# Token-shift differences on VectorE alone, and the low-rank additions behind the last receptance operand, in an RWKV-7 / NSA step

## The chip, the cores and the metric

The kernel runs on one core of a Trainium2 chip. The metric is the device time of one execution in microseconds (us). Three runs of the kernel before took 994.48, 988.21 and 993.82 us, the median is 993.82. Besides these there is one profiled execution, from which all times of single instructions come.

Engine names as in the profile: PE is TensorE (PEld its weight loads), DVE is VectorE, ACT is ScalarE, POOL is GpSimd, SP is SyncE, which issues the DMAs.

## The reference, cut to what matters

Two layers of a decoder: an RWKV-7 layer and a native-sparse-attention layer, on 512 prompt tokens and 8 x 4 sample tokens, with 1024 channels. The change lies in the first layer's beginning:

```python
hp = rms_norm(xp, norm_w[i])
prev = jnp.concatenate([shift[:, None, :], h[:, :-1]], axis=1)
xx = prev - h                                           # token shift
xr, xw, xk, xv, xa, xg = [h + xx * mu[i] for i in range(6)]
r, k, v, z = jnp.einsum('pbtc,pcd->pbtd', jnp.stack([xr, xk, xv, xg]), w_rkvz)
w = -jax.nn.softplus(-(w0 + jnp.tanh(xw @ w1) @ w2)) - 0.5    # decay
a = jax.nn.sigmoid(a0 + (xa @ a1) @ a2)                       # rate
```

After it come the recurrence over time, the gate and the output projection, and then the attention layer. Both layers' outputs and states are returned.

## The kernel before, in words

**Layout.** Activations lie with channels on the 128 partitions, in eight tiles (k = 0 to 7), and the 544 tokens along the free axis, in two halves of 272 (256 prompt tokens and 16 sample tokens each).

**Split operands.** A full-precision product is made of three products of reduced operands: each operand is a high part and a low part. `operand` (L320) calls `split` (L293): ScalarE copies the raw tile into the high part (L298), and an engine of the caller's choice subtracts it from the raw tile to give the low part (L299). `products` (L329) then runs, for every channel tile k, three matmuls a half (L337): high weight with high operand, high weight with low operand, low weight with high operand. That is 48 matmuls for an output tile of 128 channels, and those of tile k need both parts of tile k. Weights are split in the same way (`weight`, L302), their low part by GpSimd, VectorE or both in halves, as the plan's letters say (p, v, h).

**The start of layer 0** (`layer0`, L472). `rstd` (L404) computes the norm factor `rs` of every token. `low_rows` (L422) multiplies the low-rank weights of the decay and the rate straight with the raw input, once for a token's own row and once for the row before it (L446, L448), and copies the products out of PSUM on ScalarE (L452, L454). It returns a function `rows` (L456), called `hid()` in `layer0`, that finishes them on VectorE: both multiplied with `rs` (L460), and the shifted one added to the other (L461 for the prompt tokens, L462 for the first token of the second half, L465 for each of the two groups of eight sample tokens that take the given state, L466 and L467 for the other sample tokens). The result `self.hid` is read by `rates` (L604): `stack_tanh` (L538) and `stack_copy` (its first reader is L549 on ScalarE).

Then, for each channel tile k, `shifted(k)` (L507): VectorE makes the normalised tile (L510), ScalarE copies its sample tokens and writes the two edge columns (L513, L515, L516), **VectorE or GpSimd takes the difference of neighbouring tokens (L514)**, and VectorE takes the sample tokens' differences (L517). The plan's entry `shp` names the tiles whose L514 is done by GpSimd: 1, 3, 5 and 7. `mix("r", k)` (L524, VectorE) gives the receptance's mixture, and `operand(..., nc.vector)` splits it (L298 on ScalarE, L299 on VectorE).

**The loop over the eight receptance tiles** (m, from L629) loads the weights, runs `project` and copies the result out (L637). Woven into it are, at m = 1, the compression of the sample caches (`sample_pages`, L577: `cmp_bias`, L1496, with its matmuls L1505; `cmp_sample`, L1540, with its matmuls L1553 on pages that are loaded by DMA; and `cmp_hidden`, L1512, whose addition L1519 follows the copy L1517, whose product L1522 ends the hidden layer and goes to the matmul L1529); after m = 2 the call `hid()`; after each m some calls of `inputs` (L595), two each after m = 0 and m = 1, which make the mixtures of key, value and gate for a tile (L524 three times), split the first (L298, L299) and send the others to DRAM (L599); and from m = 4 the steps of `rates`.

**What sets the order.** Each engine runs its instructions in a fixed order. That order is worked out when the kernel is built, with estimated durations, from the program's order as priority: an instruction that comes later in the program may be placed ahead of an earlier one where the estimate says that the earlier one isn't ready. So the additions of `hid()`, and mixtures of `inputs`, stand on VectorE among the work on the receptance's operands, though the program names them after it. Temporary tiles come from pools of a fixed number of buffers: 8 for the raw tiles and `rs` (tag `d`), 16 for the split operands of the receptance (tag `x`), 16 shared by the key's operands and the two copies that `hid()` works on (tag `t`).

`with tc.issue_after(ins):` adds, to each instruction made in the block that runs on the engine of `ins`, an ordering behind `ins` on that engine.

Of the kernel before, what the change touches and what calls it, by code (L numbers as in the profile page):

```python
# [9 lines left out]
F32 = mybir.dt.float32  # L10
# [3 lines left out]
OP = mybir.AluOpType  # L14
# [19 lines left out]
    'FS': 4,  # L34
    'VS': (0, 0, 1, 1, 1, 1, 1, 3),
    'IV': (0, 0, 0, 0, 4, 6, 6, 0),
    'shp': (1, 3, 5, 7),
    'CS': 1,
    'FT': 1,
    'WR': 'pppvhphh',  # L40
# [186 lines left out]
class K:  # L227
# [65 lines left out]
    def split(self, raw, hi, lo, eng=None, first=None):  # L293
        nc = self.nc
        if first:
            first.tensor_copy(hi, raw)
        else:
            nc.scalar.activation(hi, raw, AF.Copy)  # L298
        (eng or nc.gpsimd).tensor_tensor(lo, raw, hi.bitcast(F32), OP.subtract)  # L299
        return hi, lo  # L300

    def weight(self, src, cols, eng=None, tag="w"):  # L302
# [96 lines left out]
    @staticmethod  # L399
    def h2(t):  # L400
        return t.rearrange("p (h n) -> p h n", h=2)
# [70 lines left out]
    def layer0(self, ctx):  # L472
        nc, I, O = self.nc, self.I, self.O
# [19 lines left out]
        for j in range(2):  # L493
            raw = self.t("p", (128, 4, 128))
# [12 lines left out]
        def shifted(k):  # L507

            h = self.t("p")
            nc.vector.scalar_tensor_tensor(h, X[k], self.V("nw0", k), rs, op0=OP.mult, op1=OP.mult)  # L510
            dx = self.t("p")
            a, d = h2(h), h2(dx)
            nc.scalar.activation(steps[:, k, 8:40].rearrange("p (h n) -> p h n", h=2), a[:, :, HP:HN], AF.Copy)  # L513
            (nc.gpsimd if k in PLAN["shp"] else nc.vector).tensor_tensor(d[:, :, 1:HP], a[:, :, 0:HP - 1], a[:, :, 1:HP], OP.subtract)  # L514
            nc.scalar.activation(d[:, 0, 0:1], a[:, 0, 0:1], AF.Copy, scale=-1.0)  # L515
            nc.scalar.activation(d[:, 1, 0:1], a[:, 1, 0:1], AF.Identity, scale=-1.0, bias=a[:, 0, HP - 1:HP])  # L516
            nc.vector.tensor_tensor(d[:, :, HP:HN], steps[:, k, 0:32].rearrange("p (h n) -> p h n", h=2),  # L517
                                    steps[:, k, 8:40].rearrange("p (h n) -> p h n", h=2), OP.subtract)
            H.append(h)
            DX.append(dx)  # L520

        def mix(n, k):
            raw = self.t("d")
            nc.vector.scalar_tensor_tensor(raw, DX[k], self.V("m" + n, k), H[k], op0=OP.mult, op1=OP.add)  # L524
            return raw
# [29 lines left out]
        def samp(dst, src, eng):  # L555
            d = dst.rearrange("p (h n) -> p h n", h=2)
            if eng is nc.scalar:
                nc.scalar.activation(d, src, AF.Copy)
            else:
                eng.tensor_copy(d, src)  # L560

        self.open(kctx, t=16, rst=1)
        hid = self.low_rows(low, X, sh, rs)
        Xr, Xk = [], []
        for k in range(KT):
            shifted(k)
            Xr.append(self.operand(mix("r", k), nc.vector))

        self.sums, self.center = (self.c0(n, (128, 128), F32R) for n in ("sums", "center"))
        self.mean = self.c("mean", (128, 128), F32R)  # L570
# [6 lines left out]
        def sample_pages():  # L577
            with ExitStack() as cctx:
                self.open(cctx, side="right", cw=1, cl=2, ca=3)
                if not PLAN["PT"]:  # L580
                    self.pages()
                if PLAN["PO"] == 0:
                    self.page_rows()
                self.cmp_weights(lambda shape: self.reg["cw"].tile(list(shape), F32, name=self.nm("cw")))
                if PLAN["PO"] == 1:
                    self.page_rows()
                self.cmp_bias()
                if PLAN["PO"] == 2:
                    self.page_rows()
                self.cmp_sample()  # L590
# [4 lines left out]
        def inputs(m):  # L595

            Xk.append(self.split(mix("k", m), self.t("t", dt=F32R), self.t("t", dt=F32R), nc.vector))
            for n in "vg":
                nc.sync.dma_start(spilled[n][:, m], mix(n, m))  # L599
            nc.scalar.activation(ps[:, m:m + 1], h2(H[m])[:, 1, HP - 1:HP], AF.Copy)  # L600
# [28 lines left out]
        for m in range(KT):  # L629
            if m == PLAN["CS"]:  # L630
                sample_pages()
            if m == 4:
                self.open(w2ctx, side="right", w2=8, st2=2)
            w = ahead[m] if m < len(ahead) else self.weight(I["rkvz"][0, m], 128, WE["WR"][m])
            pt = self.project(w, Xr)
            r = self.t("p")
            nc.scalar.activation(h2(r), pt[:, :, :HN], AF.Copy)  # L637
            samp(arS[:, m, 1], pt[:, :, HP:HN], nc.scalar)
            R.append(r)
            if m == 2:  # L640
                hid()
            for _ in range(PLAN["INP"][m]):
                inputs(len(Xk))
            if m >= 4:
                for _ in range(PLAN["RT"][m]):
                    next(rate, None)
# [1598 lines left out]
```

## Time and profile before

| | us |
|---|---|
| runs | 994.48, 988.21, 993.82 (median 993.82) |
| profiled execution, its own time | 999.77 |
| its span, first to last instruction | 997.8 |
| PE busy | 944.5 (95%) |
| DVE busy | 658.8 (66%) |
| ACT busy | 561.0 (56%) |
| POOL busy | 424.0 (42%) |
| mean granted TensorE clock | 0.974 |

How to read the rows: a row of the view in order of time has the start, the duration of the row, the engine, the source line, the operation, output and inputs, and how many instructions it merges; in brackets stands how long the engine was idle before it and what released it. A merged row's duration runs from its first start to its last end. Source lines can be those of a helper: L299 is the low part of a split, L337 a matmul of `products`. A row of the view by stretches has the stretch, its length, the busy time of PE, PEld, DVE, ACT and POOL with the number of instructions, the granted clock as a share, the DMA engines' share and GB/s. A row of the view by groups has the count, total busy time in us, the mean in ns, and the idle time before with its releasers.

### The profile page before, as it was taken

How to read it: one execution, taken by the hardware profiler on the slowest of the kernel's cores; microseconds unless marked ns; L12 is line 12 of the kernel's file. 1: busy time of each engine (PE TensorE's matmuls, PEld its weight loads, DVE VectorE, ACT ScalarE, POOL GpSimd, SP SyncE). 2: the span in 40 equal slices, each digit the busy share in tenths (PEclk: the TensorE clock that was granted, in tenths of full speed). 3: DMA queues.
4: the chain of work that ended last, by engine and by line, in shares of the span. 5: the costliest groups of instructions: out<-in, count | busy, mean ns of one | idle time of the engine just before them, and what ended most of it. 6: DMA issues, size and time to landing. Idle time of an engine off the chain costs nothing.

```text
span 997.8 us, 24773 instructions
## 1 busy us (share of the span) xinstructions
PE 944.5 (95%) x9445; PEld 845.5 (85%) x9445; DVE 658.8 (66%) x1525; ACT 561.0 (56%) x1366; POOL 424.0 (42%) x496
## 2 busy tenths in 40 slices
PE   8899999998899999999999888999999999998997
PEld 7899999988887788888879878999788888787896
DVE  6976679897847442556977624755786556569664
ACT  5455786665253353555554645656685668566552
POOL 4414646553411533421222765655343537442431
PEclk9799999999899997999999989999999999999999
DMA  5486236669374454663574795332454342555634
GB/s 191 136 274 215 87 118 188 186 192 273 112 209 117 139 138 139 208 180 94 164 222 131 247 242 168 110 109 80 123 127 136 104 123 82 155 157 187 187 103 157
DMA packets 149239, 157.46 MB, mean 158 GB/s; under 512 B 52226, under 2 KB 97058, under 8 KB 148866
## 3 DMA queue, kind: packets, MB, share of 16 engines
q1 hardware_dynamic: 149122, 155.90, 51.9%
q8 instruction: 74, 1.21, 0.5%
q14 instruction: 43, 0.35, 0.1%
HBM read 112.25 MB, written 43.80 MB: 156 GB/s over the span
## 4 chain that ended last, share of the span: by engine, by line
PE 51%; DVE 12%; DMA 7%; ACT 7%; issue 4%; POOL 3%; SPq 1%; DVEq 0%; POOLq 0%; ACTq 0%
PE ph L337 23%; PE pq L1821 4%; PE pw L1915 3%; PE pq L1899 3%; PE pr L1235 2%; DMA w<-in_win 2%; DMA d<-dram 2%; ACT l L298 2%; POOL l L299 1%; DVE tmp L1137 1%; DMA w<-in_rkvz 1%; PE ph L2167 1%; PE ph L382 1%; ACT a L1855 1%; PE s L1269 1%
## 5 line engine op out<-in xcount | busy, mean ns | idle before, releaser
L337 PE MATMUL ph<-x,l 128*128 128x272 f32 x2412 | 352.7, 297 | 6.8 <-DVE bs L680 3.0
L337 PEld LDWEIGHTS ph<-x,l 128*128 128x128 f32 x2412 | 321.3, 193 | 20.9 <-issue 6.9
L299 POOL TENSOR_TENSOR l<-w,l 128x512 fp32r<-128x512 f32 (+2 forms) x118 | 156.5, 1338 | 186.1 <-ACT l L298 153.8
L298 ACT ACTIVATE l<-w 128x512 fp32r<-128x512 f32 (+2 forms) x152 | 88.6, 611 | 102.3 <-PE ph L337 46.7
L337 PE MATMUL pp<-x,l 128*128 128x272 f32 x768 | 109.7, 296 | 4.5 <-DVE x L299 3.0
L337 PEld LDWEIGHTS pp<-x,l 128*128 128x128 f32 x768 | 101.5, 190 | 7.7 <-DVE x L299 3.6
L1855 ACT ACTIVATE a<-a,st 128x512 f32<-128x512 f32 (+3 forms) x128 | 70.7, 553 | 26.3 <-DVE st L1848 25.5
L1848 DVE CUSTOM_DVE_ANT_0 a<-pq,tb 128x512 f32<-128x512 f32 (+3 forms) x128 | 56.7, 484 | 20.9 <-PE pq L1821 20.7
L1821 PE MATMUL pq<-p,z 128*128 128x512 f32 (+7 forms) x288 | 57.7, 329 | 2.9 <-DVE st L1851 1.5
L1902 ACT ACTIVATE h<-pq 128x512 f32<-128x512 f32 x60 | 35.4, 591 | 31.4 <-PE pq L1899 27.2
L337 PE MATMUL pp<-t,l 128*128 128x272 f32 x384 | 53.0, 291 | 0.0
L1899 PE MATMUL pq<-cst,a 128*128 128x128 f32 x320 | 49.9, 277 | 3.2 <-DVE st L1851 1.8
L337 PEld LDWEIGHTS pp<-t,l 128*128 128x128 f32 x384 | 49.9, 188 | 0.5
L1821 PEld LDWEIGHTS pq<-p,z 128*128 128x128 f32 x288 | 42.5, 191 | 9.1 <-issue 5.5
L1875 DVE TENSOR_SCALAR a<-a,st 128x128 f32<-128x128 f32 (+3 forms) x112 | 49.8, 503 | 0.5
L299 POOL TENSOR_TENSOR d<-d,d 128x544 fp32r<-128x544 f32 (+2 forms) x19 | 27.7, 1459 | 42.3 <-ACT d L298 37.2
L1899 PEld LDWEIGHTS pq<-cst,a 128*128 128x128 f32 x320 | 37.5, 142 | 9.2 <-issue 5.6
L1586 DVE TENSOR_TENSOR d<-ph,RS 128x272 f32<-128x272 f32 x56 | 24.2, 437 | 29.2 <-PE ph L337 27.9
L1915 PE MATMUL pw<-h,p 128*64 128x256 f32 x320 | 38.8, 390 | 1.4 <-ACT h L1902 1.4
L299 DVE TENSOR_TENSOR l<-w,l 128x512 fp32r<-128x512 f32 x34 | 30.4, 905 | 11.4 <-ACT l L298 7.3
L724 POOL TENSOR_TENSOR d<-d,d 128x544 f32<-128x544 f32 x8 | 11.0, 1373 | 58.9 <-ACT d L396 52.9
L1235 PE MATMUL pr<-ab,ab 64*64 64x128 f32 x256 | 32.7, 275 | 1.2 <-ACT q L1221 0.7
(451 smaller groups left out, 1964.7 us busy)
## 6 DMA issues: line engine op xcount, KB each, us to landing
w<-in_rkvz SPq DMA_DIRECT2D x64, 256.0 KB, 3.5
d<-dram SPq DMA_DIRECT2D x60, 272.0 KB, 4.4
w<-in_win SPq DMA_DIRECT2D x56, 256.0 KB, 2.9
dram<-d SPq DMA_DIRECT2D x48, 272.0 KB, 3.1
ab<-dram SPq DMA_DIRECT2D x32, 256.0 KB, 4.0
p<-in_xT SPq DMA_DIRECT2D x16, 272.0 KB, 4.9
tb<-dram SPq DMA_DIRECT2D x16, 264.0 KB, 7.8
dram<-uar SPq DMA_DIRECT2D x8, 512.0 KB
```

The lines of the kernel that those rows point to most:

```text
L298: nc.scalar.activation(hi, raw, AF.Copy)
L299: (eng or nc.gpsimd).tensor_tensor(lo, raw, hi.bitcast(F32), OP.subtract)
L337: nc.tensor.matmul((pt[h][:m, :HN] if split else pt[:m, h, :HN]), a[:, k, :m], b[:, h * HN:(h + 1) * HN], start=(k == 0 and n == 0), stop= ...
L1235: nc.tensor.matmul(pg[par][r, i], BK[r, i, par], AR[r, i].rearrange("p a b -> p (a b)"), start=True, stop=True)
L1586: self.nc.vector.tensor_tensor(o, p, r, OP.mult)
L1821: nc.tensor.matmul(p[:, par], QZ[k, b][x][:, par, m], kk[:, lo:hi], start=(x == 0), stop=(x == 1))
L1848: nc.vector.tensor_tensor_reduce(out=P[par][j], in0=p[:, par, :n], in1=TB[k][:, g, o:o + n], scale=-1.0, scalar=3.0e38, op0=OP.add, op1=OP ...
L1855: nc.scalar.activation(P[par][j], P[par][j], AF.Exp, scale=-1.0, bias=st[:, 0, g, j + 1:j + 2], accum_out=st[:, 1, g, j + 1:j + 2])
L1875: (nc.gpsimd if e == "p" else nc.vector).tensor_scalar(pj, pj, rr, None, op0=OP.mult)
L1899: nc.tensor.transpose(pt[:, g % 2, g // 2], PB[g][j][:, c * 128:c * 128 + 128], ident)
L1902: nc.scalar.activation(w, pt, AF.Copy)
L1915: nc.tensor.matmul(po[r], v, W[x][:, par], start=False, stop=(x == 0), skip_group_check=True)
```

## The change

Three edits. The plan's list of tiles whose neighbour difference (L514) GpSimd takes becomes empty, so VectorE takes all eight. `split` keeps the instruction that it issued for the low part, and `layer0` notes the last receptance tile's. The call `hid()`, in its old place in the program, stands in a block that orders its instructions behind that one; they all run on VectorE, as that one does.

```diff
-    'shp': (1, 3, 5, 7),
+    'shp': (),
...
-        (eng or nc.gpsimd).tensor_tensor(lo, raw, hi.bitcast(F32), OP.subtract)
+        self.split_ins = (eng or nc.gpsimd).tensor_tensor(lo, raw, hi.bitcast(F32), OP.subtract)
         return hi, lo
...
             Xr.append(self.operand(mix("r", k), nc.vector))
+        shift_done = self.split_ins
...
             if m == 2:
-                hid()
+                with self.tc.issue_after(shift_done.ins):
+                    hid()
```

## The prediction

> **What bounds the kernel now.** I read the busy time by stretch first, then the three engines in order of time through the start of layer 0, where the change lies. The times are those of the profiled execution: 999.77 us, of which 997.8 us are the span. Columns of the first view are the stretch, its length, busy time of PE, of its weight loads, of DVE, ACT and POOL (instructions in brackets), the granted clock, the DMA share and GB/s.
>
> ```profile
> 14.00:30.00 16.00, 16.00 (x80) 13.57 (x79) 15.88 (x24) 7.63 (x32) 9.82 (x8) 1.00 0.39 111
> 51.00:70.00 19.00, 18.91 (x149) 18.39 (x148) 14.92 (x21) 9.50 (x19) 3.73 (x2) 0.97 0.81 260
> ...
> 34.00:37.40 3.40, 1.80 (x16) 1.71 (x16) 3.40 (x6) 1.46 (x6) 3.40 (x2) 1.00 0.21 31
> 38.80:51.50 12.70, 11.61 (x54) 11.31 (x53) 12.65 (x22) 4.14 (x9) 2.70 (x5) 0.50 0.34 112
> ```
>
> From 14 to 30 TensorE is full, with the low-rank products; from 51 to 70 it is full again. Between the two it is not, although DVE is busy all the time, and for some 13 us the granted clock is 0.50. So the stretch from 30 to 52 us is the place to win in: VectorE makes the receptance operands one channel tile at a time, and TensorE takes them as they come.
>
> ```profile
> 29.90 2.76 PE L337 MATMUL pp<-x,l 128*128 128x272 f32 x20
> ...
> 33.85 1.95 PE L1505 MATMUL s<-ca,cw 128*128 128x2 f32 x16
> 37.42 1.02 PE L337 MATMUL pp<-x,l 128*128 128x272 f32 x6 [1.62 <-DVE x L299]
> 38.28 2.92 PE L1553 MATMUL s<-cl,cw 128*128 128x128 f32 x14
> 42.29 1.73 PE L337 MATMUL pp<-x,l 128*128 128x272 f32 x6 [1.09 <-DVE x L299]
> 43.82 3.41 PE L1505 MATMUL s<-ca,cw 128*128 128x2 f32 x16
> 47.09 4.19 PE L1553 MATMUL s<-cl,cw 128*128 128x128 f32 x18
> 50.93 5.97 PE L337 MATMUL pp<-x,l 128*128 128x272 f32 x41
> 56.73 3.73 PE L1553 MATMUL s<-cl,cw 128*128 128x128 f32 x32
> 60.22 5.27 PE L337 MATMUL pp<-x,l 128*128 128x272 f32 x40
> ```
>
> The first receptance product is 48 matmuls: 20 from 29.90, six (not shown) at 32.95, six at 37.42, six at 42.29 and the first ten of the 41 at 50.93. The waits in brackets are for the low parts of tiles 4 and 5 (L299 on DVE). Between them TensorE runs the compression of the sample pages (L1505, L1553) in a fixed order. What the half clock costs is read from equal work: 16 matmuls of L1505 took 1.95 us before the drop and 3.41 in it; 32 of L1553 took 3.73 us at full clock, so 18 of them are 2.10, and took 4.19. Full rate for a 272-column matmul is 5.27/40 = 0.132 us. The 41 from 50.93 took 0.56 us more than 41 x 0.132, all at their beginning, so the tenth, which ends the first product, ended at about 50.93 + 1.32 + 0.56 = 52.8. That is the mark I reckon by.
>
> **VectorE's chain.** First one undisturbed round of the work for a tile, and one stalled instruction on either side; then the end of the chain, with the low-rank additions in it; then GpSimd's side.
>
> ```profile
> 19.96 1.55 DVE L524 SCALAR_TENSOR_TENSOR d<-p,vec,p 128x544 f32<-128x544 f32 x1
> ...
> 21.54 0.68 DVE L514 TENSOR_TENSOR p<-p 128x510 f32<-128x510 f32 x1
> 22.14 0.77 DVE L510 SCALAR_TENSOR_TENSOR p<-p,vec,d 128x544 f32<-128x544 f32 x1
> 22.84 0.18 DVE L517 TENSOR_TENSOR p<-steps 128x32 f32<-128x32 f32 x1
> 22.94 0.77 DVE L524 SCALAR_TENSOR_TENSOR d<-p,vec,p 128x544 f32<-128x544 f32 x1
> 23.64 0.71 DVE L299 TENSOR_TENSOR x<-d,x 128x544 fp32r<-128x544 f32 x1
> 24.27 1.55 DVE L510 SCALAR_TENSOR_TENSOR p<-p,vec,d 128x544 f32<-128x544 f32 x1
> ...
> 34.11 0.72 DVE L460 TENSOR_TENSOR t<-t,d 128x544 f32<-128x544 f32 x1
> 34.75 1.29 DVE L517 TENSOR_TENSOR p<-steps 128x32 f32<-128x32 f32 x1
> ...
> 37.29 0.71 DVE L460 TENSOR_TENSOR t<-t,d 128x544 f32<-128x544 f32 x1
> 37.93 1.06 DVE L517 TENSOR_TENSOR p<-steps 128x32 f32<-128x32 f32 x1
> 38.91 1.51 DVE L465 TENSOR_TENSOR t<-t,first 64x8 f32<-64x8 f32 x2
> ...
> 42.16 0.68 DVE L461 TENSOR_TENSOR t<-t,t 128x510 f32<-128x510 f32 x1
> ...
> 42.83 3.56 DVE L524 SCALAR_TENSOR_TENSOR d<-p,vec,p 128x544 f32<-128x544 f32 x5
> 46.31 0.15 DVE L466 TENSOR_TENSOR t<-t,t 128x8 f32<-128x8 f32 x1
> ...
> 46.47 0.78 DVE L524 SCALAR_TENSOR_TENSOR d<-p,vec,p 128x544 f32<-128x544 f32 x1
> 47.16 0.71 DVE L299 TENSOR_TENSOR x<-d,x 128x544 fp32r<-128x544 f32 x1
> ...
> 48.49 0.72 DVE L299 TENSOR_TENSOR x<-d,x 128x544 fp32r<-128x544 f32 x1
> ```
>
> ```profile
> L514 POOL TENSOR_TENSOR p<-p 128x510 f32<-128x510 f32 x4 | 9.0, 2258 | 6.2 <-DVE p L517 3.5 <-DVE p L510 2.7
> ```
>
> ```profile
> 22.99 2.25 POOL L514 TENSOR_TENSOR p<-p 128x510 f32<-128x510 f32 x1 [2.06 <-DVE p L510]
> ...
> 38.90 1.26 POOL L299 TENSOR_TENSOR l<-w,l 128x512 fp32r<-128x512 f32 x1
> ```
>
> Starts lie closer than durations, so the cost of an instruction on the engine is the step from its start to the next: 0.60 us for a difference (L514, 21.54 to 22.14), 0.70 for L510, 0.10 for L517, 0.70 for a mix (L524), 0.63 for a low part (L299). And a DVE instruction that meets one on GpSimd stands: the mix at 19.96 and the L510 at 24.27 took 1.55 us instead of 0.77, the 32-column difference at 37.93 took 1.06 instead of 0.18, the one at 34.75 1.29. The stall at 24.27 lies within GpSimd's difference that runs from 22.99 to 25.24. The low part of the last tile is done at 48.49 + 0.72 = 49.21.
>
> **The differences go to VectorE.** Removed: four instructions of GpSimd (9.0 us there, which nobody misses, since GpSimd's own next work waits for others) and the stalls that they give DVE: 0.78, 0.78 and 0.88 in the three shown, 0.81 on average, 3.25 for four. Added: four times 0.60 = 2.4 us on DVE, in its path. Net 0.85 us gained on the chain if all four stalls go with their cause, 2.4 us lost if none goes (GpSimd's other work would have to cause them). I take the gain, since the stalled instruction at 24.27 stands just while that difference runs. The bounds are +2.4 and -0.85.
>
> **The additions go behind the last low part.** Removed from the chain, by steps of starts: two products with the norm factor (L460), 0.64 each; the two additions of eight columns (L465), 1.51 measured, of which 0.2 are theirs by the step of L517 and 1.3 the stall against GpSimd's weight split at 38.90, which will hit whatever stands there instead; L461 with the single-column L462 0.67, to 42.83; the last two (L466, L467) 0.16, from 46.31 to 46.47. Sum 2.31 us, up to 3.6 if the stall went too. I take 2.3. These eight instructions don't vanish: they come after 49.21 less the gain, on a DVE that is still full then. Who waits for their result are the decay's and rate's inputs, first on ACT:
>
> ```profile
> 66.10 0.66 ACT L549 ACTIVATE d<-t 64x544 f32<-64x544 f32 x1
> ```
>
> That is 17 us after 49, and the eight take some 3: DVE's other work until 61 covers them, and without that cover they would cost their 2.3 us there. They bring no DMAs and they wait for nothing new, because their inputs are long there; the buffer of the norm factor and two operand buffers are held some us longer.
>
> So the last low part moves from 49.21 to 49.21 - 0.85 - 2.31 = 46.05. The mixes for the inputs of the other projections, four of the five at 42.83 and two more up to 48.49, stand ahead of it today. Six times 0.70 is 4.2: it would be 41.9 if the order, made anew when the kernel is built, put them behind. I leave them where they are, and keep 41.9 as the other end.
>
> **TensorE with these times.** The low part of tile 4 gains 0.64 and up to 0.6 from the swaps: six matmuls start at about 36.5 and not 37.42. They take 0.86 (37.42 to 38.28), to 37.4; 14 of L1553 at full clock 1.6, to 39.0. The low part of tile 5 gains 0.64 + 0.64 + 0.2 + 0.85 = 2.3, to 40.0; its matmuls to 40.9; L1505 1.95, to 42.8; 18 of L1553 2.1, to 44.9. Then tile 6, and tile 7's last four after 46.05: 46.6, against 52.8. That is 6.2 us, if the clock stays up. Of these only about 3.2 are VectorE's; the rest is matmuls that need not run at 0.50. Why it should stay up: before the drop TensorE had only the two-column matmuls and the wait from 33.85 to 37.42, 3.57 us without a wide matmul; here it is about 2.7.
>
> [...]
>
> **What comes back.** After the mark TensorE is full (18.91 of 19 us), so an earlier start there lasts, unless something that VectorE makes is late for it. The first such thing is the hidden layer of the compressed pages:
>
> ```profile
> 58.33 2.42 DVE L299 TENSOR_TENSOR t<-d,t 128x544 fp32r<-128x544 f32 x2
> 61.13 0.65 DVE L1519 TENSOR_TENSOR ca<-s,ca 64x480 f32<-64x480 f32 x1 [0.37 <-ACT ca L1517]
> ```
>
> ```profile
> 66.11 0.65 DVE L1522 TENSOR_TENSOR ca<-ca,ca 64x480 f32<-64x480 f32 x1 [1.71 <-ACT ca L396]
> ...
> 69.68 1.07 PE L1529 MATMUL s<-ca,cw 64*128 64x480 f32 x2
> ```
>
> DVE's unbroken work ends at 60.75 and would end at 59.9, because the additions only move within it. L1519 then starts 1.2 sooner than 61.13, and L1522 ends at 65.5 and not 66.76. TensorE, 6.2 ahead, would want it at 63.5: 2.0 us lost if the order is as now, none if L1519 is put ahead of the last mixes. I take 1.0. Forecast: 6.2 - 1.0 = 5.2 us. The profiled execution would go from 999.77 to 994.6; on the median of the runs, 993.82, it is 988.6.
>
> **Rivals.**
> *The clock falls all the same* (0.20). For it: L1505 still stands between tiles 4 and 5 and is thin work. Against: shorter gaps. The matmuls from tile 5 to the mark keep their old durations, and only tile 5's 2.3 us are gained; L1522 has 2.9 us to spare (66.76 to 69.68), so nothing is given back: 991.5.
> *Larger* (0.15): the input mixes fall behind, the last low part is there at 41.9, and TensorE alone sets the pace: from 32.66 on 0.86 + 1.95 + 0.86 + 1.6 + 0.86 + 1.95 + 2.1 + 1.3 = 11.5, to 44.2, which is 8.6 less than 52.8, with L1519 put in time: 985.2.
> *The move does nothing* (0.13): the room that the additions leave is filled with more of the mixes (four are 2.8 us, the gain 3.2), and the low parts come when they did: 993.8. For it: such fillers stand in the chain today. Against: their buffers are few, and one is now held longer.
> *Slower* (0.10): the stalls don't go with the differences. Then DVE has 2.4 us more ahead of tile 4, 0.64 less for the addition: the six matmuls at 37.42 come up to 1.8 us later, the thin stretch is 5.3 us instead of 3.57, and the clock falls sooner by what the stretch grew. That is 1.8 us of matmuls at half rate, 0.9, and the 1.8 us themselves, and up to 0.8 more at L1519: 997.3. It decides from the point where tile 4's low part is later than 37.4. Against: the stall rows.
>
> **How the numbers follow.** The forecast has 0.42, and 986 to 991 as its own range. From 985.2 to 997.3 the cases reach; below, I add 3.2 us, half of the distance of the three runs (988.21 to 994.48), because an order made anew may also move later stages: 982 to 997. A measurement tells about 1% (9.9 us) from no change. Faster than that needs the larger case with another 1.3 us from somewhere (half of 0.15) or the forecast with twice its gain (0.07 of its 0.42): 0.15. Slower by over 1% needs half of the slower case, and a little for later stages: 0.06. Within 1%: 0.79.
>
> **What would show it.** Right: no L514 on GpSimd; L510 and L524 at 0.77 us in that stretch; L460 to L467 after the last low part; that part at about 46; a granted clock of 1.00 from 38 to 52; the end of the first product near 46.6; L1519 near 60, and TensorE idle ahead of L1529 by up to 2 us. Wrong: stalls of 1.55 us that stay, a last low part at 49 or later, a clock of 0.50 in the middle, or an earlier mark with the end of the span where it was; in that last case the time is given back after 70 us, at a wait that I haven't found.

## The result, and the profile after

The changed kernel takes 1005.53 us (median of 1007.11, 1003.95, 1011.03 and 1003.1), the kernel before beside it 993.52 (median of 988.21 to 994.48, four runs). The ratio is 1.0106, with a 95% interval of 1.0072 to 1.0140: slower by some 10 to 12 us, where 5.2 us of gain were forecast. Ratios here and below leave out single slow runs (over 1.5% above the fastest of the same kernel), which the medians contain, and are not the quotients of the medians beside them. The profiled execution of the changed kernel took 1007.11 us, with a span of 1005.3 and a granted clock of 0.977 (before: 999.77, 997.8, 0.974). Line numbers of the changed kernel are one higher from L568 and two higher from L641 (L1505 is L1507, L1519 is L1521, L1529 is L1531, L1553 is L1555).

Most of what was forecast for the start came about. The stretches of the changed kernel, in the same columns as before:

```profile
14.00:30.00 16.00, 16.00 (x80) 13.57 (x79) 15.89 (x26) 8.17 (x34) 4.63 (x5) 1.00 0.38 112
51.00:70.00 19.00, 19.00 (x151) 18.10 (x150) 16.18 (x30) 10.03 (x19) 0.57 (x1) 1.00 0.90 294
34.00:37.40 3.40, 2.41 (x20) 2.31 (x20) 3.37 (x3) 2.82 (x13) 3.01 (x2) 1.00 0.24 79
38.80:51.50 12.70, 12.70 (x100) 12.70 (x99) 12.70 (x18) 5.89 (x13) 5.08 (x5) 0.90 0.67 200
```

TensorE, which was busy for 1.80 of 3.40 us and then ran 54 instructions at half clock, now runs 100 in the same 12.70 us, at a clock of 0.90. VectorE and GpSimd in order of time:

```profile
35.89 1.79 DVE L299 TENSOR_TENSOR x<-d,x 128x544 fp32r<-128x544 f32 x1
37.61 0.68 DVE L514 TENSOR_TENSOR p<-p 128x510 f32<-128x510 f32 x1
...
44.09 0.71 DVE L299 TENSOR_TENSOR x<-d,x 128x544 fp32r<-128x544 f32 x1
44.72 1.35 DVE L460 TENSOR_TENSOR t<-t,d 128x544 f32<-128x544 f32 x2
...
54.62 0.17 DVE L467 TENSOR_TENSOR t<-t,t 128x16 f32<-128x16 f32 x1
...
59.45 0.64 DVE L1521 TENSOR_TENSOR ca<-s,ca 64x480 f32<-64x480 f32 x1
```

```profile
33.96 3.15 POOL L299 TENSOR_TENSOR l<-w,l 128x512 fp32r<-128x512 f32 x2 [15.33 <-DMA w<-in_rkvz]
40.73 0.54 POOL L574 CAST sums<-d 128x128 fp32r<-128x128 f32 x1 [3.62 <-DMA d<-in_heads]
```

The differences are on VectorE and none on GpSimd; the last low part is done at 44.09 + 0.71 = 44.8 us (49.21 before); the additions follow it, from 44.72 to 54.8; the hidden layer's L1521 starts at 59.45 (61.13 before). TensorE:

```profile
41.67 1.00 PE L337 MATMUL pp<-x,l 128*128 128x272 f32 x6
42.51 1.84 PE L1507 MATMUL s<-ca,cw 128*128 128x2 f32 x16
44.21 1.14 PE L1555 MATMUL s<-cl,cw 128*128 128x128 f32 x8
45.10 3.00 PE L337 MATMUL pp<-x,l 128*128 128x272 f32 x22
...
67.89 1.07 PE L1531 MATMUL s<-ca,cw 64*128 64x480 f32 x2
```

The prediction's mark, the tenth projection matmul after tile 5's six, is at 45.10 + 10 x 0.132 = 46.4 us; 46.6 was forecast, and 52.8 was the profile of before. But the hidden layer's matmul is only 1.8 us earlier (67.89 against 69.68), and the span ends 7.5 us later. So the loss lies behind the stretch that the prediction worked out, and behind the instructions that the change edits.

### The profile page after: what moved, and what is told of

Read it like the earlier page. It is cut to its first block, busy times and chain, and to the rows that moved or that the text cites. A ratio compares the mean times of both kernels' runs of the same rounds, so it can differ in the third digit from the quotient of the medians.

```text
span 1005.3 us, 24763 instructions
## 1 busy us (share of the span) xinstructions
PE 945.2 (94%) x9445; PEld 844.0 (84%) x9445; DVE 655.8 (65%) x1529; ACT 560.4 (56%) x1366; POOL 409.8 (41%) x492
## 4 chain that ended last, share of the span: by engine, by line
PE 49%; DVE 8%; ACT 5%; DMA 3%; issue 2%; POOL 1%; SPq 1%; DVEq 0%; ACTq 0%; POOLq 0%
PE ph L337 22%; PE pq L1823 3%; PE pw L1917 3%; PE pq L1901 3%; PE pr L1237 2%; PE ph L2169 1%; ACT a L1857 1%; PE ph L382 1%; ACT l L298 1%; DVE a L1877 1%; PE pr L1289 1%; PE s L1253 1%; DMA tb<-dram 1%; PE ph L1434 1%; PE pr L1286 1%
## 5 line engine op out<-in xcount | busy, mean ns | idle before, releaser
L337 PE MATMUL ph<-x,l 128*128 128x272 f32 x2412 | 352.0, 297 | 5.8 <-DVE bs L682 1.7
L337 PEld LDWEIGHTS ph<-x,l 128*128 128x128 f32 x2412 | 320.7, 192 | 19.0 <-issue 7.6
L299 POOL TENSOR_TENSOR l<-w,l 128x512 fp32r<-128x512 f32 (+2 forms) x118 | 153.9, 1317 | 206.4 <-ACT l L298 163.5
L337 PE MATMUL pp<-x,l 128*128 128x272 f32 x768 | 112.4, 300 | 3.2 <-DVE bs L682 2.9
L337 PEld LDWEIGHTS pp<-x,l 128*128 128x128 f32 x768 | 103.7, 195 | 5.8 <-issue 3.0
L337 PE MATMUL pp<-t,l 128*128 128x272 f32 x384 | 54.1, 292 | 0.0
L337 PEld LDWEIGHTS pp<-t,l 128*128 128x128 f32 x384 | 50.3, 188 | 0.6
L1917 PEld LDWEIGHTS pw<-h,p 128*64 128x64 f32 x320 | 22.0, 139 | 13.5 <-ACT h L1904 2.2
```

Of the source, the lines that this page charges most:

```text
L299: self.split_ins = (eng or nc.gpsimd).tensor_tensor(lo, raw, hi.bitcast(F32), OP.subtract)
L337: nc.tensor.matmul((pt[h][:m, :HN] if split else pt[:m, h, :HN]), a[:, k, :m], b[:, h * HN:(h + 1) * HN], start=(k == 0 and n == 0), stop= ...
L1917: nc.tensor.matmul(po[r], v, W[x][:, par], start=False, stop=(x == 0), skip_group_check=True)
```

## Where the loss appears

The table counts the projection matmuls (L337, 3564 in each trace) in order of time, and gives how much earlier (-) or later (+) the Nth starts than in the profile of before. The kernels on the right are explained with the experiments: "late order held" is the change with before's order behind the receptance tiles, "old order held" the change with before's order from the receptance operands on, "new order" is the kernel before with the changed kernel's later order, and the last two are again the kernel before.

| N (time before) | changed | late order held | old order held | new order | before, again | before, again |
|---|---|---|---|---|---|---|
| 100 (62.8) | -6.4 | -7.8 | -3.7 | -3.3 | -3.6 | -3.5 |
| 500 (134.5) | -2.3 | -1.2 | -0.6 | +1.4 | -1.2 | -3.3 |
| 600 (151.1) | -2.7 | -1.2 | -0.6 | +0.9 | -1.2 | -3.3 |
| 1000 (220.4) | +3.7 | -1.1 | -1.0 | +5.6 | -2.2 | -4.1 |
| 1400 (339.2) | -0.8 | -1.5 | 0.0 | +4.2 | -3.6 | -5.3 |
| 1600 (485.3) | +4.2 | -1.8 | +0.1 | +14.7 | -4.6 | -5.5 |
| 1800 (536.5) | +8.6 | -2.0 | +0.2 | +20.4 | -4.5 | -5.5 |
| 2400 (646.8) | +9.5 | -3.0 | -0.8 | +22.1 | -1.8 | -6.1 |
| 3500 (958.4) | +7.3 | -2.5 | -0.6 | +19.7 | -3.2 | -7.4 |

The changed kernel loses 6 us between 151 and 220 us; some of it comes back by 339, and 10 more are lost by 647. These are the keys' and values' part of layer 0 and the recurrence's, whose code the change doesn't touch. What differs there is the order. It is made anew when the kernel is built, and of the instructions that the program names after the eight receptance tiles another one stands in the place at 2262 of 6507 positions on TensorE, 366 of 1287 on VectorE, 270 of 1065 on ScalarE, 54 of 464 on GpSimd and 151 of 666 on SyncE.

## The experiments

Four explanations were to be told apart, in the order in which they came up. *The later order*: the changed code itself gains or does nothing, and the order made anew costs the time. *The start itself*: what the change does in the first 60 us costs it (the additions late for ScalarE, a buffer held longer). *The page loads*: the gain at the start is real and is given back at once, because the sample pages' loads stand on SyncE's queue behind stores of mixtures that don't come sooner. *The clock*: a large part of the forecast gain was never there, because the half clock in the profile of before was longer than it usually is.

To hold an order, a table of positions for each engine is put at the end of the kernel, and each instruction in it gets an ordering behind the one before it on its engine, which adds no wait across engines (shortened: the import and the string `ORDER` are left out, and `NoSync` stands for the kind of edge that orders two instructions and waits for no semaphore):

```diff
-    k.layer1()
+    k.layer1(); pin(nc, tc, first)
...
+def pin(nc, tc, first):
+    traced = nc.cur_bb.bb.instructions
+    at = next(n for n, i in enumerate(traced) if i.name == first)
+    for line in zlib.decompress(base64.b85decode(ORDER)).decode().split(";"):
+        n, prev = at, None
+        for d in line.split(",") if line else ():
+            n += int(d)
+            if prev is not None:
+                tc.add_manual_dep(traced[n], prev.name, NoSync, reason="pin")
+            prev = traced[n]
```

The kernels differ in `ORDER` (from the build of before or of the changed kernel), in `first` (the end of the receptance tiles, or of their operands), and in the change's own edits. All ratios are against the kernel before on the same chip (median there 997.1, 996.19 and 999.11 us in the three sets of timed runs below).

**Is it the later order or the start?** The change with before's order behind the receptance tiles (`both_old_order`), the kernel before with the changed kernel's order there (`none_new_order`), and each half of the change alone, its order left to the build.

```diff
 both_old_order: the change, and
+    k.layer1(); pin(nc, tc, "I-1529")     # ORDER of before
 none_new_order: before, and
+    k.layer1(); pin(nc, tc, "I-1529")     # ORDER of the changed kernel
 differences_alone: before, and
-    'shp': (1, 3, 5, 7),
+    'shp': (),
 additions_alone: before, and
+        shift_done = self.split_ins
...
-                hid()
+                with self.tc.issue_after(shift_done.ins):
+                    hid()
```

> The change as it is, but everything that the program names after the eight receptance tiles is held, engine by engine, in the order that it had in the kernel before. Theory 1 (the start gains its 6 us and the new order of the later instructions, which the build makes as a side effect, loses 15 or more): 986 to 990, that is 4 to 7 us below the kernel before, and the two traces keep a constant distance from 130 us on. Theory 2 (the start itself leaves something behind that costs later, such as late low-rank rows or transfers that collide, whatever the later order): 1000 to 1006, as the change.

> The kernel before, with nothing of the change in its start, but everything named after the receptance tiles held in the order that it has in the changed kernel. Theory 1: slower than the kernel before by 10 us or more, 1003 to 1012, that is the change's time and the 6 us that its start gains on top. Theory 2: within 3 us of the kernel before, 991 to 996.

> Only the first part: all eight differences on VectorE, the low-rank additions free as before. The order of all that is named after the receptance tiles comes out the same as in the changed kernel. Theory 1: slower than the kernel before, since that order is what costs, and 2 to 5 us above or at the change: 1003 to 1010; the last low part near 48.4 (49.2 less 0.85). Theory 2, if the fault is in the rows that come late: as before or better, 990 to 994.

> Only the second part: the additions behind the last low part, four differences on GpSimd as before. The order of all that is named after the receptance tiles again comes out the same as in the changed kernel. Theory 1: 1003 to 1010, the last low part near 46.9 (49.2 less 2.3). Theory 2 with the late rows at fault: as the change, 1003 to 1006; with the differences at fault: as the kernel before.

| kernel | median us (runs) | ratio, 95% interval |
|---|---|---|
| both_old_order | 996.54 (12) | 0.9997, 0.9967 to 1.0026 |
| none_new_order | 1015.45 (6) | 1.0158, 1.0103 to 1.0212 |
| differences_alone | 1010.66 (6) | 1.0101, 1.0054 to 1.0148 |
| additions_alone | 1014.37 (6) | 1.0166, 1.0120 to 1.0212 |

With before's order behind the receptance tiles the change costs nothing that can be measured; the new order alone, with nothing of the change, costs 1.0158, some 15.8 us (18 by the medians). Each half of the change brings the very same later order as the whole (no position differs), and each is slower by about as much. That settles the loss: it is the order. The first run came out between its two expectations: the loss went, but the 4 to 7 us of gain that the first theory promised with it weren't there. The other three came 1 to 4 us above the first theory's ranges. Stretches of before (first fence), of the changed kernel (second), and of the kernel that has only the new order (third):

```profile
160.00:200.00 40.00, 39.47 (x357) 37.19 (x356) 33.37 (x53) 25.07 (x47) 21.98 (x30) 1.00 0.61 183
400.00:420.00 20.00, 20.00 (x326) 17.15 (x323) 10.05 (x22) 12.17 (x29) 7.43 (x6) 1.00 0.71 211
```

```profile
160.00:200.00 40.00, 35.40 (x325) 32.98 (x324) 27.50 (x48) 25.06 (x45) 19.29 (x29) 1.00 0.57 177
400.00:420.00 20.00, 18.37 (x329) 16.23 (x326) 9.34 (x20) 9.11 (x21) 2.75 (x3) 1.00 0.46 135
```

```profile
160.00:200.00 40.00, 35.31 (x322) 32.81 (x322) 27.54 (x46) 22.15 (x40) 19.05 (x29) 1.00 0.59 178
400.00:420.00 20.00, 18.36 (x305) 16.15 (x301) 8.32 (x18) 8.74 (x21) 2.62 (x2) 1.00 0.32 97
```

TensorE, full there before, has 4.6 us of 40 and 1.6 of 20 empty, and nearly the same in both kernels with the new order. The waits say what is late: from 150 to 245 us, then from 440 to 560. Columns are who waits for whom, microseconds in all, times, and the longest. First the changed kernel:

```profile
PE pp L337 <- DVE bs L682: 2.9, 2, 2.1
PE pr L1047 <- DVE p L1029: 2.2, 2, 1.4
PE pr L1026 <- DVE ubk L1101: 0.9, 1, 0.9
...
PE s L1253 <- DVE q L1243: 1.8, 1, 1.8
PE pr L1229 <- ACT q L1223: 1.6, 1, 1.6
```

Then the kernel with the new order alone:

```profile
PE pp L337 <- DVE bs L680: 2.8, 2, 2.0
PE pr L1045 <- DVE p L1027: 2.0, 2, 1.3
...
PE s L1251 <- DVE q L1241: 1.8, 1, 1.8
PE pr L1227 <- ACT q L1221: 1.6, 1, 1.6
```

In the profile of before the first of these is 1.5 us, the second 0.6, and the last two aren't there or are 0.5. They aren't one wait that grew but many small ones. Where they are longer, VectorE or ScalarE gives a result later than TensorE's order wants it; that it is their place on the queue was not tried one by one.

The waits are not the whole loss. All that the view lists for the two stretches sums to 2.7 and 6.0 us before, and to 7.0 and 7.5 with the new order alone (7.4 and 7.9 in the changed kernel): 6 us more of some 16. TensorE is also busy for longer with the same 9445 instructions: 954.7 us with the new order alone, 944.5 before (938.1 and 939.0 in the two repeats of it, below). The granted clock of the new order alone is lower, 0.967 over the span against 0.974 before (0.981 and 0.978 in the repeats, 0.977 in the changed kernel); in one stretch, before, then the changed kernel, then the new order alone:

```profile
400.00:520.00 120.00, 116.61 (x1847) 99.03 (x1843) 82.55 (x213) 65.03 (x160) 33.12 (x37) 1.00 0.59 174
400.00:520.00 120.00, 113.16 (x1735) 95.34 (x1731) 76.16 (x193) 61.12 (x150) 30.75 (x33) 0.99 0.53 151
400.00:520.00 120.00, 113.76 (x1669) 96.86 (x1664) 68.25 (x179) 55.15 (x137) 28.32 (x30) 0.91 0.51 149
```

In this stretch the clock is 1.00 in all nine profiles with before's late order, and 0.90 to 0.99 in all five with the new one. In the timed runs the mean clock is 0.970 with the new order alone and 0.980 for the kernel before beside it, and among runs of either kernel 0.01 less goes with 7 to 9 us more. A straight line of time against clock through both, an estimate from these runs, gives the new order 9.3 us (7 to 12) at equal clock; the other 8 go with the lower clock. What in the new order brings the clock down isn't shown.

**Which part of the order, and the start with everything held.** The new order only from the end of the receptance products to the end of the keys and values (`middle_new_order`), or only behind that (`late_new_order`), both on the kernel before; and the change (`both_all_old_order`) or its differences alone (`differences_all_old_order`) with everything behind the receptance operands in before's order, but for the eight additions in the first of the two, which stay where the change puts them.

```diff
 middle_new_order, late_new_order: before, and
+    k.layer1(); pin(nc, tc, "I-1529")     # ORDER mixed of both
 both_all_old_order: the change, differences_all_old_order: 'shp' alone, and
+    k.layer1(); pin(nc, tc, "I-377")      # ORDER of before
```

> The kernel before with the new order only for what the program names from the end of the receptance products to the end of the keys and values (reached at some 245 us), the old order for the rest. In the trace of the kernel with the whole new order, some 5 us were lost between 160 and 220 us, and part of it came back by 255. Theory 1 with both parts costly: 3 to 6 us above the kernel before. With the cost in the later part alone: within 2 us.

> The kernel before with the old order up to the end of the keys and values and the new order for all that the program names after them. The trace of the kernel with the whole new order lost some 6 us between 364 and 427 us and 9 more by 532. Theory 1: 10 to 16 us above the kernel before, most of the 15.8 us of the whole new order. If the loss needed the earlier part's order too: within 5 us.

> The change, and everything that the program names after the receptance operands (the receptance products, the sample pages, the inputs of the other projections and the low-rank rates too, but not the eight additions) is held in the order that it had in the kernel before, on every engine. The run with only the later order held gained 8 us by the hundredth projection matmul and had 2 left 50 us later. Theory 1b (that return, too, is a matter of order, in this nearer part: four casts of the small weights now stand ahead of the decay's stack): the gain stays, 5 to 8 us below the kernel before, 989 to 992 against 997. Theory 3 (the pages and weights that DMAs bring limit an earlier TensorE, in any order): waits for the transfers in 55 to 100 us, and 0 to 3 us below the kernel before at the end.

> The first part alone, with everything after the receptance operands held in the old order, the additions included (they stand where they stood). Theory 1b: the chain of VectorE gains 0.85, the first product ends 1 to 4 us sooner as the clock falls out, and this stays: 0 to 4 us below the kernel before. Theory 3: 0 to 1 us below. If the stalls had not gone with the differences: 1 to 3 us above.

| kernel | median us (runs) | ratio, 95% interval |
|---|---|---|
| middle_new_order | 1000.89 (12) | 1.0024, 0.9998 to 1.0050 |
| late_new_order | 1010.22 (6) | 1.0124, 1.0086 to 1.0163 |
| both_all_old_order | 996.78 (12) | 0.9989, 0.9964 to 1.0014 |
| differences_all_old_order | 997.20 (12) | 1.0001, 0.9979 to 1.0024 |

The two parts of the order add up to the whole (0.0024 + 0.0124 = 0.0148 against 0.0158): most of it, some 12 us, lies behind the keys and values, the rest isn't told from nothing. And the start is worth nothing that can be measured, also with everything behind it held: of the two expectations for that run the one of 0 to 3 us came true, not the one of 5 to 8. At equal clock, by the same estimate, the change is at -0.6 us (-2.0 to 0.9) with the late order held and at -0.3 (-1.7 to 1.1) with everything held; 5.2 us of gain lie outside both. That spoke against the forecast gain, not only for a cost elsewhere.

**Is the gain given back, or was it never there?** Before with its order held on itself, which is the same program, profiled twice more; and the change and before with 11 of the pages' loads moved ahead of the stores of mixtures in SyncE's order (the first of the twelve that the expectation names stood ahead of them already).

```diff
 before_again_1, before_again_2: before, and
+    k.layer1(); pin(nc, tc, "I-1529")     # ORDER of before: nothing changes
 both_pages_first: both_all_old_order, before_pages_first: before, and
+    # in SyncE's line of ORDER, 11 loads cl<-in_cck, cl<-in_ccv ahead of the stores of L599/L600
```

> The kernel before, its order held on itself, so the same program: another profile. If the time at half clock (13 us in the first profile) is a draw of the single execution, it will differ here, and with it the end of the first receptance product (52.8 us in the first profile): 49 to 53. The runs with the unchanged start showed the hundredth projection matmul 2 to 3 us sooner than the first profile, so 50 is the likelier value, and then the gain of the start against a usual execution is 3 us smaller than it looked.

> The same once more, for the same reason: the end of the first receptance product between 49 and 53, the half clock between 0 and 13 us.

> The change with everything after the receptance operands in the old order, but for SP's queue: twelve page loads of the sample caches stand ahead of the stores of mixtures between which they stood. In the run without this edit the loads came behind stores that waited for VectorE's mixtures, and TensorE waited 0.5 + 0.9 us for pages between 54 and 75. Theory 3 (what an earlier TensorE gains is lost to transfers behind those stores): the waits for pages by 62 us go, the lead after 100 us grows by 1 to 2.5 us, and the time falls by as much, 1 to 4 us below the kernel before. Theory 4 (VectorE's unbroken work to 60 us, which the change shortens by under 1 us, holds everything after it, whatever the queue): another wait, for a result of VectorE or for a later transfer, takes the place; the lead after 100 us stays at 0.5 to 1.5 us, and the time within 1.5 us of the kernel before.

> The control: the kernel before with the same twelve page loads moved ahead in SP's queue. TensorE had no wait for pages in the kernel before until 75 us, so both theories expect no change beyond 1.5 us, unless the stores, now later, hold up the mixtures' buffers (then up to 2 us slower).

The two repeats took 996.68 and 992.31 us (one run each, spans 994.6 and 990.5). The first of them, the kernel before, TensorE and then VectorE in order of time:

```profile
37.31 1.73 PE L337 MATMUL pp<-x,l 128*128 128x272 f32 x6 [1.62 <-DVE x L299]
38.83 2.37 PE L1553 MATMUL s<-cl,cw 128*128 128x128 f32 x14
42.18 1.02 PE L337 MATMUL pp<-x,l 128*128 128x272 f32 x6 [0.97 <-DVE x L299]
43.04 1.84 PE L1505 MATMUL s<-ca,cw 128*128 128x2 f32 x16
44.74 2.25 PE L1553 MATMUL s<-cl,cw 128*128 128x128 f32 x18
46.75 5.40 PE L337 MATMUL pp<-x,l 128*128 128x272 f32 x41
...
66.50 1.07 PE L1529 MATMUL s<-ca,cw 64*128 64x480 f32 x2
```

```profile
41.16 0.97 DVE L299 TENSOR_TENSOR x<-d,x 128x544 fp32r<-128x544 f32 x1
...
48.39 0.71 DVE L299 TENSOR_TENSOR x<-d,x 128x544 fp32r<-128x544 f32 x1
...
60.49 0.64 DVE L1519 TENSOR_TENSOR ca<-s,ca 64x480 f32<-64x480 f32 x1
```

And the changed kernel with everything held (`both_all_old_order`), the same two views:

```profile
39.10 3.04 PE L1555 MATMUL s<-cl,cw 128*128 128x128 f32 x14
41.90 1.00 PE L337 MATMUL pp<-x,l 128*128 128x272 f32 x6
42.74 1.84 PE L1507 MATMUL s<-ca,cw 128*128 128x2 f32 x16
44.44 2.25 PE L1555 MATMUL s<-cl,cw 128*128 128x128 f32 x18
46.45 5.38 PE L337 MATMUL pp<-x,l 128*128 128x272 f32 x41
...
66.42 1.07 PE L1531 MATMUL s<-ca,cw 64*128 64x480 f32 x2
```

```profile
39.22 0.71 DVE L299 TENSOR_TENSOR x<-d,x 128x544 fp32r<-128x544 f32 x1
...
44.24 0.71 DVE L299 TENSOR_TENSOR x<-d,x 128x544 fp32r<-128x544 f32 x1
...
50.90 2.48 DVE L465 TENSOR_TENSOR t<-t,first 64x8 f32<-64x8 f32 x2
...
60.33 0.65 DVE L1521 TENSOR_TENSOR ca<-s,ca 64x480 f32<-64x480 f32 x1
```

VectorE's last low part comes 4.15 us sooner (48.39 to 44.24), and TensorE's 41 matmuls start 0.30 sooner, L1531 0.08. In the first repeat of before, TensorE runs its 41 matmuls at full rate from 46.75 (5.40/41 = 0.132 us each), although the last low part is done only at 49.10: the last operand wasn't what TensorE stood for. The mark of the repeats (46.75 + 1.32 = 48.1, and 48.5 in the second) lies just below the 49 to 53 expected.

The pages' loads moved ahead: `before_pages_first` takes 995.78 us (12 runs), a ratio of 0.9963 (0.9928 to 0.9998), `both_pages_first` 995.52 (12 runs), 0.9977 (0.9945 to 1.0008). The kernel before gains by it at least as much as the changed one, where no more than 1.5 us had been expected of it, so nothing of the change is seen to be hidden behind these loads. The first of the two, which has nothing of the change, is the only version here that measures faster than the kernel before, by some 3.7 us, at the edge of its interval. That it is the wait for pages which got shorter isn't shown: between 50 and 80 us TensorE waits 2.7 us for them in its profile, and 1.7 in the first repeat of before.

## Why the prediction was wrong

Two steps failed. The gain of 6.2 us was measured from a mark that was late in that one profile, for a last operand that TensorE doesn't stand for. And the order made anew, which the sum has at nothing, costs more than the whole forecast gain.

**VectorE's chain: right at its end, wrong at tile 4.** The last low part was to move from 49.21 to 46.05 and came at 44.8 (44.95 with the order held). Of the 1.3 us more, two of the six mixtures for other projections that stood ahead make up all (0.70 each): they now stand behind it. The prediction had all six behind as its other end. Tile 4's low part was to gain 0.64 us or more and start TensorE's six matmuls at about 36.5; they start at 37.74 in the changed kernel and 37.96 with the order held, later than the 37.42 of before. The differences' stalls went with them: L510 and L524 take 0.77 or 0.78 us from 19.86 to 33.64 in the changed kernel, where before has three of 1.55 in that time. Those against GpSimd's weight splits stayed, as the prediction had it for the 1.3 us at L465, in other places: in the changed kernel the low part at 35.89 took 1.79 us and not 0.71, beside GpSimd's splits from 33.96 to 37.11 (this is tile 4's), and with the order held the two L465 took 2.48 us at 50.90 (0.33 in the changed kernel), beside splits from 50.75 to 53.36. VectorE's unbroken work was to end 0.85 us sooner; L1521 starts 0.16 sooner with the order held and 1.0 in the changed kernel, against the 60.49 of the first repeat.

**The mark at 46.6: right; what it was measured from: wrong.** The first step that failed is "ended at about 50.93 + 1.32 + 0.56 = 52.8. That is the mark I reckon by". Of the 6.2 us, 3 were put down to matmuls that "need not run at 0.50", as if the half clock of 13 us belonged to the kernel. It belonged to that execution. The same program, profiled again, has the mark at 48.1 and 48.5. The granted clock from 38.8 to 51.5 us in the first repeat:

```profile
38.80:51.50 12.70, 11.73 (x94) 11.54 (x93) 12.65 (x22) 4.52 (x10) 2.58 (x5) 0.95 0.47 151
```

That is 0.95 where the profile of before has 0.50, after the same stretch on TensorE (3.57 us without a wide matmul in both, 1.62 of them idle). Against these marks the changed kernel's 46.4 is 1.7 to 2.1 us, and with the order held (46.45 + 1.3 = 47.8) 0.3 to 0.7. Nor did the clock stay up in the changed kernel, as it was to: 0.90. That a shorter stretch without a wide matmul keeps the clock up, as the 6.2 us have it, or that a longer one lets it fall sooner, as the rival for slower has it, was the author's estimate from one profile, and no run shows it. The longest such stretch between 33 and 38 us was 1.82 us in the changed kernel (34.02 to 35.84) and 2.78 with the order held (35.18 to 37.96), and the clock from 38 to 52 us was 0.88 in both; with 3.57, 3.57 and 3.58 in three executions of the kernel before it was 0.52, 0.92 and 0.81. Nor does the tenth matmul end the first product, as the prediction has it. In the order of before, matmuls of another receptance tile stand between, and the product ends with the 28th of the 41: at 50.4 and 50.8 in the repeats, and at about 55.1 in the profile of before. In the changed kernel it ends with the 16th after tile 5's six, at 47.2, because the new order puts its matmuls ahead.

**The last low part as what TensorE waits for: wrong.** TensorE has work from other products to put between, and it runs through: in the first repeat the tenth of the 41 ends at 48.1, and tile 7's low part, done at 49.10, is first taken by the 25th, at about 49.9. What stood in its way were the operands of tiles 4 and 5 and the clock; tile 5's came 2.2 us sooner (41.16 + 0.97 = 42.13 in the first repeat, 39.22 + 0.71 = 39.93 with the order held; 2.3 was forecast). TensorE couldn't use it: the 14 matmuls of L1555 ahead of that tile's six started at 39.10, behind the late tile 4, and took 3.04 us, where 1.6 is their time at full clock (14/32 of the 3.73 us that L1553 took at 56.73 in the profile of before, at 1.00; here the clock was 0.66 from 37 to 42 us), so the six started at 41.90 against 42.18.

**"An earlier start there lasts": wrong.** The hidden layer's matmul is at 66.50 and 66.39 in the repeats of before, 66.42 with the order held, and 67.89 in the changed kernel. With the order held, the 0.3 to 0.7 us of the mark are gone by then; in the changed kernel 1.7 us ahead at the mark have become 1.4 behind, against the first repeat, with 41 more projection matmuls put ahead of the hidden layer's in its order. The forecast gave 1.0 us back here.

A lead can be had, and is lost further on. In the profile of `both_old_order` the clock stayed at 1.00 from 38 to 52 us, and its 100th projection matmul comes some 4 us ahead of the repeats; its 500th, at 134 us, is no earlier than theirs. Between 60 and 135 us TensorE waits 1.3 us there for pages and 1.2 for the hidden layers, and for the decay's and rate's products

```profile
PE pr L618 <- DVE st L388: 2.5, 1, 2.5
```

where the first repeat has 1.1 us of waits in all, for pages. L388 makes the low part of their operand, from the result of `hid()`. In that kernel, whose order is free up to the end of the receptance tiles, four casts of weights (L296, 4.72 us from 90.11) stand ahead of it on VectorE, and the copy that it needs (L387) starts at 92.21 on ScalarE, behind a weight split that waited 3.15 us for its load; in the first repeat the copy starts at 88.07, ahead of that split. The changed kernel has the same wait, of 1.2 us. So here a wait does give time back, as the prediction's last sentence allowed for; that holding this nearer order too would keep the lead isn't shown, because with everything held there was none at the 100th matmul.

**"An order made anew may also move later stages": mis-sized.** This is the second step that failed. The forecast has it at nothing; the range has 3.2 us for it on the faster side alone, and the upper end, 997, none; the chance for slower has "a little". It was 15.8 us alone (1.0158), and in the changed kernel it is the whole loss: with before's order behind the receptance tiles the ratio is 0.9997. That is why the range, 982 to 997, missed. The wrong outcome was foreseen in words ("the time is given back after 70 us, at a wait that I haven't found"), without a price. That the rival for slower (stalls that stay) had a mechanism didn't help: that mechanism isn't what made the kernel slower.

**What stays open.** Given the new order on both sides, the change reads 1.0106 against 1.0158, some 5 us better; given the old order, 0.9989 against 1. The intervals overlap, and the timed runs had a clock of 0.977 on average for the one and 0.970 for the other, so part of the 5 us is the clock. A gain of a microsecond or two is neither shown nor excluded. Nor was it tried which single position of the later order costs most, or brings the clock down; the waits shown are spread over several places.

## What to carry to other kernels

Where the order of instructions is made when the kernel is built, an edit of the first 50 us is two changes, the edit and a new order everywhere behind it; compare the orders first, hold the old one to see the edit alone, and give the new order its own term and its own range (here some 16 us of 997). A stretch at half clock in one profile is not a cost of the kernel until a second execution shows it as well (here 0.50 in one and 0.95 in the next). And an engine that is idle before an operand need not be waiting for the last operand of the row (here that came 4.15 us sooner and TensorE's matmuls 0.30): see whether its next matmuls run through without it.

## What the runs showed of the hardware

The granted clock after one and the same idle stretch differed between executions: from 38 to 52 us it was 0.52, 0.92 and 0.81 in three executions of the kernel before, and 0.80, 0.65 and 0.91 in the three kernels that keep its start (the new order alone, in the middle, and late). Spans of the one program went from 990.5 to 997.8 us. So a difference of 7 us between two single profiles is no finding here; it takes timed runs. The clock differed with the order as well: from 400 to 520 us it was 1.00 in nine profiles with one late order and 0.90 to 0.99 in five with the other.
